# Gate weights on VectorE, staggered first tiles, and value products of 288 and 144 columns in an mLSTM block

## The chip, the cores and the metric

One NeuronCore of a Trainium2 chip runs the whole program. The time is device microseconds of one execution, from the first to the last instruction and what lies around them; 2079.76 us is the median of three runs. TensorE (PE) multiplies, with its weight loads shown apart (PEld), VectorE (DVE), ScalarE (ACT) and GpSimd (POOL) do the elementwise work, and SyncE (SP) issues the DMAs.

## What is computed

Two layers on 1024 latent tokens and 256 context tokens of width 1024. The change lies in the first layer, a bidirectional mLSTM. Its features and gates are, cut to what matters:

```python
xm, z, og = split(h @ w_in, 3)            # h: 1280 tokens x 1024, each part 2048 wide
xc = silu(short_conv(xm, conv_w, conv_b)) # width 3 along the tokens
q = headwise(xc, w_q); k = headwise(xc, w_k) * DH ** -0.5
v = headwise(xm, w_v)                     # blocks of 4 channels
pre = concat(q, k, v) @ w_gate + b_gate   # 16 gate columns: both directions
# then the chunked scans of both directions over 4 heads, norm, gating with z and og, @ w_out
```

The second layer is a pooling mixer; the change does not touch it.

## The kernel before

Float32 accuracy comes from products of two halves: each operand is a high part and a low part in float32r, and mm3 makes high x high, high x low and low x high into one PSUM buffer. So each operand is split: ACT copies the high part, DVE subtracts it from the value for the low part.

**Start.** ada_product and ada_turn make shift and scale for 128 columns of the width at a time; PE_START is the order, written out by hand, of these steps and of the steps F0 to F7. F k is early(k): it modulates column tile k of the normalized input, splits it, and multiplies it with the weights of the first two of 16 feature tiles (n = 0 and 1). Each of the two tiles has three PSUM buffers, for 512, 512 and 256 tokens.

**Feature tiles.** For each n, features(n, side) makes 128 channels of xm: three token chunks of 8 x 3 matmuls. Each chunk is copied to xp for the convolution (L367), its high part to xmh (L369) and its low part to xml (L370); then the convolution (L372 to L374), silu (L375), the split into xch and xcl (L382, L383), and stores. token_part(n) is a generator that features(n+1) and (from n = 1 on: two of them in features(2)) later tiles draw on through `next(side)`, between their own groups of matmuls: after every group for n = 2, after every second one else. A step multiplies 128 tokens of xm with vv, the 128 columns of the block-diagonal v weights and 16 gate columns (144 together), as high and low; three such steps share a PSUM buffer of tag "pb" (two buffers), and ACT and DVE then read it for v's high part (L409), its low part (L410) and the gate sums `pre` (L411). The last step adds the gate products of xch and xcl (tag "pc").

**gate_weights** multiplies the gate weights into the 4x4 blocks of q, k and v and leaves them, split, in gx_all and gm_all; vv takes its 16 columns from gm_all (L397). It is called behind features(1) and runs on POOL; its three tiles of weights are loaded into buffers of tag "T5" (five buffers).

**block_sums** prepares sums of blocks of h for the Strassen products behind the feature tiles. For each of four k it loads two tiles of h_d (L511), forms the sums (L513 to L516), and in four further steps splits one each (L520, L521) and stores it. Two steps are taken behind each feature tile from n = 2 on. All of these tiles, and xmh, xml, xch and xcl, have tag "S4" (32 buffers).

**Order.** PE's order in this stage is the program's. On the other engines and the queues a planner puts the instructions in order before the run, by its own timeline; each engine then works its list in order. Buffers of a tag pass from one tile to the next.

**Plain and Strassen products** for z and og follow (L528 on); the first plain product draws the rest of token_part(15). Then the heads: start_head(0) loads chunk 0 of xh_d and xl_d of the first head (fetch_x), make_A and next_q make q, load_ctx_gates and load_gates fetch the gates' rows, finish_x loads chunks 1 and 2, and fetch_v the values. score_chunk(st, ci) multiplies q with chunk ci.

Of the kernel before, what the change touches and what calls it, by code (L numbers as in the profile page):

```python
# [51 lines left out]
def hybrid_block(ctx: ExitStack, tc: tile.TileContext, xT, ctxT, vecs, w_ada0, w_ada, w_blk, w_krow, blk_mask, w_gate, w_in, b_gate, w_out,  # L52
# [219 lines left out]

    ps_, quad = {}, []

    def early(k):
# [13 lines left out]
        for n in range(2):  # L289
            if k == 0:  # L290
                ps_[n] = [pt_("pc" if n else "pa") for _ in range(3)]
            for ci in range(3):
                mm3(ps_[n][ci][:, :CHUNKS[ci][1]], first_w[n][0][:, k], first_w[n][1][:, k], hx(k, ci, 0), hx(k, ci, 1),
                    k == 0, k == KD - 1)
# [25 lines left out]
    def gate_weights():  # L320
        gsum = tl("T5", [P, 3, KE, 16])

        def add4(dst, src):
            G.tensor_tensor(dst, src[:, :, 0], src[:, :, 1], op=ALU.add)
            for o in (2, 3):
                G.tensor_tensor(dst, dst, src[:, :, o], op=ALU.add)

        for i in range(3):
            g4 = tl("T5", [P, KE, 4, 16])
            nc.sync.dma_start(g4, w_gate[i])  # L330
            G.tensor_tensor(g4, g4, wb[:, i, :, :, None].to_broadcast([P, KE, 4, 16]), op=ALU.mult)
            add4(gsum[:, i], g4)
        G.tensor_scalar(gsum[:, 1], gsum[:, 1], QSCALE, None, op0=ALU.mult)
        G.tensor_tensor(gsum[:, 0], gsum[:, 0], gsum[:, 1], op=ALU.add)
        for dst, i in ((gx_all, 0), (gm_all, 2)):
            G.tensor_copy(dst[:, :, 0:16], gsum[:, i])
            G.tensor_tensor(dst[:, :, 16:32], gsum[:, i], f(dst[:, :, 0:16]), op=ALU.subtract)
# [14 lines left out]
    def features(n, side):  # L352
# [7 lines left out]
        for ci, (o, w) in enumerate(CHUNKS):  # L360
# [9 lines left out]
            V.tensor_tensor(dl, p[:, :w], f(dh), op=ALU.subtract)  # L370
# [18 lines left out]
    def token_part(n, xmh, xml, xch, xcl):  # L389
# [8 lines left out]
        vh, vl = tl("T5", [P, 10, P], F32R), tl("T5", [P, 10, P], F32R)  # L398
        for s0, s1 in ((0, 3), (3, 6), (6, 9), (9, 10)):
            p = pt_("pb", [P, 3, 144])  # L400
            for s in range(s0, s1):
# [5 lines left out]
                mm3(p[:, s - s0], ah, al, vv[:, 0], vv[:, 1], True, True)  # L407
            q = p[:, :s1 - s0]
            S.activation(vh[:, s0:s1], q[:, :, :P], AF.Copy)  # L409
            V.tensor_tensor(vl[:, s0:s1], q[:, :, :P], f(vh[:, s0:s1]), op=ALU.subtract)  # L410
            V.tensor_tensor(pre[:, s0:s1], pre[:, s0:s1], q[:, :, P:], op=ALU.add)  # L411
        for t, dst in ((vh, vh_d), (vl, vl_d)):
            nc.sync.dma_start(dst[n // 4, :, :, (n % 4) * P:(n % 4 + 1) * P], f(t))
# [112 lines left out]
    with ctx0:  # L526
        for n in range(KE):
# [8 lines left out]
            if n >= 2:  # L536
                for _ in range(2):
                    next(sums, None)
# [739 lines left out]
```

## Time and profile before

| | us |
|---|---|
| median of 3 runs (2079.72 to 2080.05) | 2079.76 |
| the profiled execution | 2081.2 |
| its span, first to last instruction | 2079.4 |
| PE busy in the span | 1993.0 (96%) |
| PE busy from 0 to 260 us | 209.6 |
| feature tile without a disturbance | 18.4 |
| feature stage, 88.3 to 393.0 us | 304.7 |

A row of a stretch gives the busy time of each engine, the number of its instructions, and the granted clock of TensorE as a share of full speed (2.4 GHz). A timeline row is start, duration, engine, line, operation, output and inputs, and in brackets how long the engine had been idle before and what ended that. Matmuls overlap; the distance of two starts tells what one costs.

### The profile page before, as it was taken

To read this page: it belongs to the slowest core of one execution; us is meant where nothing else is said; L and a number is where in the kernel's file an instruction comes from. 1 tells how busy PE (TensorE), PEld (TensorE's weight loads), DVE (VectorE), ACT (ScalarE), POOL (GpSimd) and SP (SyncE) were. 2 spreads that over 40 slices of the span, in tenths; PEclk is the share of its full clock that TensorE was granted. 3 is DMA by queue.
4 is the path that set the end of the run, shared out by engine and by line. 5 is a ranking of instruction groups with operands and counts; after the bars stand their busy time and mean duration, and the time that the engine had idled before them with its cause. 6 is when DMAs were issued, how large, how long until landed. Compare 5 with 4: busy or idle time off the path is not lost.

```text
span 2079.4 us, 26941 instructions
## 1 busy us (share of the span) xinstructions
PE 1993.0 (96%) x10210; PEld 1681.9 (81%) x10210; DVE 1232.9 (59%) x2106; ACT 759.7 (37%) x1225; POOL 309.1 (15%) x394
## 2 busy tenths in 40 slices
PE   6779999999999899999999999999999999999998
PEld 4567888878888678888888888887888888888897
DVE  4636666677777666667676572454647283744444
ACT  5424555433333332333323332443423131224443
POOL 1120000033223000000000000252100000000275
PEclk9889999999999999999999999999999999999999
DMA  8347776774443674737447234534331212134573
GB/s 349 125 146 246 252 247 234 246 269 140 136 147 127 209 250 123 254 107 244 137 138 247 94 99 137 175 131 150 122 112 51 96 51 86 57 106 142 174 246 127
DMA packets 201986, 339.48 MB, mean 163 GB/s; under 512 B 12508, under 2 KB 116444, under 8 KB 201856
## 3 DMA queue, kind: packets, MB, share of 16 engines
q1 hardware_dynamic: 201856, 337.76, 48.0%
q8 instruction: 80, 1.31, 0.3%
q14 instruction: 50, 0.41, 0.1%
HBM read 234.77 MB, written 102.94 MB: 162 GB/s over the span
## 4 chain that ended last, share of the span: by engine, by line
PE 84%; DMA 5%; DVE 4%; POOL 3%; issue 2%; ACT 1%; SPq 0%; DVEq 0%; POOLq 0%; ACTq 0%
PE pa L136 43%; PE pc L136 32%; PE pb L136 7%; PE pb L787 1%; DMA wr<-in_w_ada_dram 1%; POOL S L995 1%; POOL hn L975 1%; PE pc L818 1%; DMA S<-in_w_ada_dram 1%; DMA S<-in_ctxT_dram 0%; DVE wl L664 0%; DVE S L907 0%; DMA T<-in_bw_out_dram 0%; DMA S<-xl_d 0%; DVE T L746 0%
## 5 line engine op out<-in xcount | busy, mean ns | idle before, releaser
L136 PE MATMUL pa<-S,wh 128*128 128x512 f32 (+1 forms) x2448 | 709.8, 375 | 5.3 <-DVE pt L370 5.0
L136 PEld LDWEIGHTS pa<-S,wh 128*128 128x128 f32 x2448 | 437.9, 190 | 75.0 <-DVE pt L370 5.6
L136 PE MATMUL pc<-S,wh 128*128 128x512 f32 (+1 forms) x1664 | 464.5, 365 | 3.9 <-ACT wh L142 3.1
L136 PE MATMUL pa<-S,wl 128*128 128x512 f32 (+1 forms) x1224 | 453.5, 371 | 3.9 <-DVE wl L144 3.9
L136 PEld LDWEIGHTS pc<-S,wh 128*128 128x128 f32 x1664 | 301.2, 189 | 55.1 <-ACT wh L142 3.3
L144 DVE TENSOR_TENSOR wl<-wr,wh 128x1024 fp32r<-128x1024 f32 (+1 forms) x124 | 147.3, 1188 | 271.3 <-ACT wh L142 270.4
L136 PE MATMUL pc<-S,wl 128*128 128x512 f32 (+1 forms) x832 | 302.3, 365 | 1.0 <-DVE wl L144 1.0
L136 PEld LDWEIGHTS pa<-S,wl 128*128 128x128 f32 x1224 | 232.4, 190 | 44.8 <-DVE wl L144 4.7
L136 PE MATMUL pa<-S,S 128*128 128x512 f32 (+1 forms) x1152 | 251.1, 363 | 10.0 <-DMA S<-xh_d 6.3
L142 ACT ACTIVATE wh<-wr 128x1024 fp32r<-128x1024 f32 (+1 forms) x124 | 124.7, 1006 | 362.7 <-PE pa L136 142.4
L136 PE MATMUL pc<-S,pt 128*128 128x512 f32 x960 | 227.8, 392 | 1.3 <-DVE S L727 0.9
L136 PEld LDWEIGHTS pa<-S,S 128*128 128x128 f32 x1152 | 191.9, 190 | 40.1 <-DMA S<-xh_d 6.7
L136 PEld LDWEIGHTS pc<-S,pt 128*128 128x128 f32 x960 | 178.4, 188 | 38.4 <-DVE S L727 1.6
L136 PEld LDWEIGHTS pc<-S,wl 128*128 128x128 f32 x832 | 157.3, 189 | 26.6 <-DVE wl L144 1.8
L789 ACT ACTIVATE pt<-pb 128x512 fp32r<-128x512 f32 (+1 forms) x96 | 47.9, 523 | 215.3 <-PE pb L787 209.5
L975 POOL TENSOR_TENSOR hn<-hn,pt 128x512 f32<-128x512 f32 (+1 forms) x48 | 77.5, 1617 | 308.5 <-ACT pt L974 307.4
L746 DVE SCALAR_TENSOR_TENSOR T<-pa,T 128x256 f32<-128x256 f32 (+3 forms) x184 | 78.1, 453 | 33.7 <-PE pa L136 29.5
L136 PEld LDWEIGHTS pb<-vv,S 128*128 128x128 f32 x384 | 62.8, 194 | 37.6 <-issue 26.0
L136 PE MATMUL pb<-vv,S 128*128 128x144 f32 x384 | 59.6, 265 | 27.2 <-DVE vv L397 25.6
L136 PE MATMUL pb<-S,wh 128*128 128x512 f32 x256 | 78.8, 389 | 0.0
L576 ACT ACTIVATE wh<-T 128x512 fp32r<-128x512 f32 x70 | 41.2, 627 | 96.3 <-PE pc L136 78.4
L410 DVE TENSOR_TENSOR T<-pb,T 128x384 fp32r<-128x384 f32 x64 | 31.3, 490 | 72.8 <-ACT T L409 72.7
(323 smaller groups left out, 2317.5 us busy)
## 6 DMA issues: line engine op xcount, KB each, us to landing
wr<-in_bw_in_dram SPq DMA_DIRECT2D x40, 512.0 KB, 3.6
wr<-in_w_in_dram SPq DMA_DIRECT2D x34, 512.0 KB, 4.7
wr<-in_w_ada_dram SPq DMA_DIRECT2D x32, 512.0 KB, 4.2
wr<-in_w_out_dram SPq DMA_DIRECT2D x32, 512.0 KB, 3.6
T<-in_bw_out_dram SPq DMA_DIRECT2D x32, 512.0 KB, 4.6
S<-y_d SPq DMA_DIRECT2D x28, 512.0 KB, 7.1
vh_d<-T SPq DMA_DIRECT2D x16, 640.0 KB, 4.0
vl_d<-T SPq DMA_DIRECT2D x16, 640.0 KB, 5.6
```

The lines of the kernel that those rows point to most:

```text
L136: PE.matmul(out, lhsT, rhs, start=start, stop=stop)
L142: S.activation(h, r, AF.Copy)
L144: V.tensor_tensor(l, r, f(h), op=ALU.subtract)
L410: V.tensor_tensor(vl[:, s0:s1], q[:, :, :P], f(vh[:, s0:s1]), op=ALU.subtract)
L576: S.activation(hi, a, AF.Copy)
L746: V.scalar_tensor_tensor(W[:, lo + sh:hi + sh], p[:, lo - o:hi - o], 1.0, W[:, lo + sh:hi + sh], op0=ALU.mult, op1=ALU.mult, accum_out=dp[ ...
L787: PE.transpose(p[:, j], st["M"][:, s * P:(s + 1) * P], ident)
L789: S.activation(th[:, :n], p[:, :n], AF.Copy)
L818: PE.transpose(p[:, c], hn[:, c * P:(c + 1) * P], ident)
L975: G.tensor_tensor(acc, acc, sq, op=ALU.add)
L995: engs[1].tensor_tensor(t, t, xr[n // per][:, n % per], op=ALU.add)
```

## The change

Six edits. In the start, tile 1 runs four column tiles behind tile 0 and catches up at k = 7. gate_weights is called ahead of features(0) and runs on VectorE. L370 reads xp in place of the PSUM buffer. A value step multiplies the high part of the tokens with both halves of vv at once (288 columns), adds the low part's product to the first half (144 columns), and has a PSUM buffer of its own, copied by ACT; for five token tiles at once DVE then adds the two halves and the gate sums, and v is split and stored. block_sums has a sixth step, ahead of the sums, and three steps are taken per tile up to n = 9. At the start of the heads, chunk 1 of head 0 is fetched right behind chunk 0, and load_gates stands ahead of load_ctx_gates.

```diff
@@ -286,12 +287,17 @@
             parts = [(*pair, slice(0, T))]
         modulate(x_sb[k], rs_xs, parts, k, 0, h_d[k])
         modulate(c_sb[k // 4][:, k % 4], rs_cs, [(hch[k // 4][:, k % 4], hcl[k // 4][:, k % 4], slice(0, TC))], k, 1)
-        for n in range(2):
-            if k == 0:
-                ps_[n] = [pt_("pc" if n else "pa") for _ in range(3)]
-            for ci in range(3):
-                mm3(ps_[n][ci][:, :CHUNKS[ci][1]], first_w[n][0][:, k], first_w[n][1][:, k], hx(k, ci, 0), hx(k, ci, 1),
-                    k == 0, k == KD - 1)
+        feature_step(0, k)
+        for k1 in (k - 4,) if k < KD - 1 else range(3, KD):
+            if k1 >= 0:
+                feature_step(1, k1)
+
+    def feature_step(n, k):
+        if k == 0:
+            ps_[n] = [pt_("pc" if n else "pa") for _ in range(3)]
+        for ci in range(3):
+            mm3(ps_[n][ci][:, :CHUNKS[ci][1]], first_w[n][0][:, k], first_w[n][1][:, k], hx(k, ci, 0), hx(k, ci, 1),
+                k == 0, k == KD - 1)
 
     rows = {}
     for step in PE_START.split():
@@ -321,20 +327,20 @@
         gsum = tl("T5", [P, 3, KE, 16])
 
         def add4(dst, src):
-            G.tensor_tensor(dst, src[:, :, 0], src[:, :, 1], op=ALU.add)
+            V.tensor_tensor(dst, src[:, :, 0], src[:, :, 1], op=ALU.add)
             for o in (2, 3):
-                G.tensor_tensor(dst, dst, src[:, :, o], op=ALU.add)
+                V.tensor_tensor(dst, dst, src[:, :, o], op=ALU.add)
 
         for i in range(3):
             g4 = tl("T5", [P, KE, 4, 16])
             nc.sync.dma_start(g4, w_gate[i])
-            G.tensor_tensor(g4, g4, wb[:, i, :, :, None].to_broadcast([P, KE, 4, 16]), op=ALU.mult)
+            V.tensor_tensor(g4, g4, wb[:, i, :, :, None].to_broadcast([P, KE, 4, 16]), op=ALU.mult)
             add4(gsum[:, i], g4)
-        G.tensor_scalar(gsum[:, 1], gsum[:, 1], QSCALE, None, op0=ALU.mult)
-        G.tensor_tensor(gsum[:, 0], gsum[:, 0], gsum[:, 1], op=ALU.add)
+        V.tensor_scalar(gsum[:, 1], gsum[:, 1], QSCALE, None, op0=ALU.mult)
+        V.tensor_tensor(gsum[:, 0], gsum[:, 0], gsum[:, 1], op=ALU.add)
         for dst, i in ((gx_all, 0), (gm_all, 2)):
-            G.tensor_copy(dst[:, :, 0:16], gsum[:, i])
-            G.tensor_tensor(dst[:, :, 16:32], gsum[:, i], f(dst[:, :, 0:16]), op=ALU.subtract)
+            V.tensor_copy(dst[:, :, 0:16], gsum[:, i])
+            V.tensor_tensor(dst[:, :, 16:32], gsum[:, i], f(dst[:, :, 0:16]), op=ALU.subtract)
 
     gx_all = tl("hn", [P, KE, 32], F32R)
     gm_all = tl("hn", [P, KE, 32], F32R)
@@ -367,7 +373,7 @@
             S.activation(xp[:, xo:xo + w], p[:, :w], AF.Copy)
             dh, dl = (xmh[0][:, o:o + w], xml[0][:, o:o + w]) if ci < 2 else (xmh[1], xml[1])
             S.activation(dh, p[:, :w], AF.Copy)
-            V.tensor_tensor(dl, p[:, :w], f(dh), op=ALU.subtract)
+            V.tensor_tensor(dl, xp[:, xo:xo + w], f(dh), op=ALU.subtract)
         y = tl("T5", [P, 1281])
         S.activation(y, xp[:, 1:1282], AF.Identity, scale=vc("conv_w", 16 + n), bias=vc("conv_b", n))
         V.scalar_tensor_tensor(y, xp[:, 0:1281], vc("conv_w", n), y, op0=ALU.mult, op1=ALU.add)
@@ -395,22 +401,24 @@
         V.tensor_copy(vv[:, 0, :P], bv)
         V.tensor_tensor(vv[:, 1, :P], bv, f(vv[:, 0, :P]), op=ALU.subtract)
         V.tensor_copy(vv[:, :, P:], f(gm_all[:, n]).rearrange("p (a b) -> p a b", a=2))
-        vh, vl = tl("T5", [P, 10, P], F32R), tl("T5", [P, 10, P], F32R)
-        for s0, s1 in ((0, 3), (3, 6), (6, 9), (9, 10)):
-            p = pt_("pb", [P, 3, 144])
-            for s in range(s0, s1):
+        for s0 in (0, 5):
+            vst, vhl = tl("T5", [P, 2, 5, 144]), tl("T5", [P, 2, 5, P], F32R)
+            for s in range(s0, s0 + 5):
                 yield
                 if s < 8:
                     ah, al = xmh[0][:, s * P:(s + 1) * P], xml[0][:, s * P:(s + 1) * P]
                 else:
                     ah, al = xmh[1][:, (s - 8) * P:(s - 7) * P], xml[1][:, (s - 8) * P:(s - 7) * P]
-                mm3(p[:, s - s0], ah, al, vv[:, 0], vv[:, 1], True, True)
-            q = p[:, :s1 - s0]
-            S.activation(vh[:, s0:s1], q[:, :, :P], AF.Copy)
-            V.tensor_tensor(vl[:, s0:s1], q[:, :, :P], f(vh[:, s0:s1]), op=ALU.subtract)
-            V.tensor_tensor(pre[:, s0:s1], pre[:, s0:s1], q[:, :, P:], op=ALU.add)
-        for t, dst in ((vh, vh_d), (vl, vl_d)):
-            nc.sync.dma_start(dst[n // 4, :, :, (n % 4) * P:(n % 4 + 1) * P], f(t))
+                p = pt_("pb", [P, 2, 144])
+                mm(p.rearrange("p a b -> p (a b)"), ah, vv.rearrange("p a b -> p (a b)"), True, False)
+                mm(p[:, 0], al, vv[:, 0], False, True)
+                S.activation(vst[:, :, s - s0], p, AF.Copy)
+            V.tensor_tensor(vst[:, 0], vst[:, 0], vst[:, 1], op=ALU.add)
+            V.tensor_tensor(pre[:, s0:s0 + 5], pre[:, s0:s0 + 5], vst[:, 0, :, P:], op=ALU.add)
+            S.activation(vhl[:, 0], vst[:, 0, :, :P], AF.Copy)
+            V.tensor_tensor(vhl[:, 1], vst[:, 0, :, :P], f(vhl[:, 0]), op=ALU.subtract)
+            for t, dst in ((vhl[:, 0], vh_d), (vhl[:, 1], vl_d)):
+                nc.sync.dma_start(dst[n // 4, :, s0:s0 + 5, (n % 4) * P:(n % 4 + 1) * P], f(t))
         yield
 
         gx = gx_all[:, n]
@@ -509,6 +517,7 @@
             t0, t1 = tl("S4", [P, T]), tl("S4", [P, T])
             for t, kk in ((t0, k), (t1, k + 4)):
                 nc.sync.dma_start(t, h_d[kk])
+            yield
             b11, b12, b21, b22 = t0[:, :512], t0[:, 512:], t1[:, :512], t1[:, 512:]
             V.scalar_tensor_tensor(b22, b22, dsh[:, k], b12, op0=ALU.add, op1=ALU.subtract)
             V.tensor_tensor(b12, b12, b11, op=ALU.subtract)
@@ -524,17 +533,17 @@
 
     side, parts, sums = iter(()), [], block_sums()
     with ctx0:
+        gate_weights()
         for n in range(KE):
             out = features(n, side)
             for _ in side:
                 pass
             if n == 1:
                 gacc.extend(pt_("pc") for _ in range(3))
-                gate_weights()
             if n == 2:
                 bilinear()
             if n >= 2:
-                for _ in range(2):
+                for _ in range(3 if n < 10 else 2):
                     next(sums, None)
             parts.append(token_part(n, *out))
             if n:
@@ -839,10 +848,11 @@
             fetch_x(cur["hd"], cur["h"], ci)
 
     cur = start_head(0)
+    fetch_x(cur["hd"], 0, 1)
     cur["A"] = make_A(0)
     cur["q"] = next_q(cur, 0)
-    cur["rc"], cur["R"] = load_ctx_gates(0), load_gates(0)
-    finish_x(cur)
+    cur["R"], cur["rc"] = load_gates(0), load_ctx_gates(0)
+    fetch_x(cur["hd"], 0, 2)
     fetch_v(cur["hd"], 0, 0, 5)
     st_prev = st_now = nxt = None
     for i in range(len(seq) + 1):
```

## Rows read from the trace of the kernel before

**Rows 1.** Page, part 1: busy us (share) and instructions of each engine.

```profile
PE 1993.0 (96%) x10210; PEld 1681.9 (81%) x10210; DVE 1232.9 (59%) x2106; ACT 759.7 (37%) x1225; POOL 309.1 (15%) x394
```

**Rows 2.** Waits of PE, whole run: us in total, times, longest.

```profile
PE pb L136 <- DVE vv L397: 25.6, 1, 25.6
...
PE pa L136 <- DMA S<-xh_d: 6.3, 1, 6.3
...
PE pa L136 <- DMA S<-xl_d: 1.9, 1, 1.9
...
PE pa L136 <- DVE S L727: 1.8, 1, 1.8
```

**Rows 3.** Stretches: busy us per engine, PEclk, DMA share, GB/s.

```profile
88.30:139.80 51.50, 25.35 (x144) 21.13 (x145) 24.97 (x42) 17.59 (x29) 18.45 (x24) 0.73 0.43 149
...
158.20:184.40 26.20, 22.44 (x111) 18.34 (x110) 16.18 (x30) 11.94 (x22) 0.15 (x3) 0.87 0.57 202
...
239.80:261.00 21.20, 18.37 (x108) 15.51 (x106) 11.82 (x23) 9.95 (x16) 0.15 (x3) 0.98 0.82 264
261.00:282.50 21.50, 21.45 (x109) 18.20 (x110) 13.27 (x26) 10.32 (x18) 0.15 (x3) 0.86 0.56 205
...
337.80:356.20 18.40, 18.40 (x109) 15.82 (x108) 10.52 (x21) 9.22 (x17) 0.16 (x3) 1.00 0.58 200
```

**Rows 4.** Timeline of POOL: first and last operation of gate_weights.

```profile
96.88 2.32 POOL L331 TENSOR_TENSOR T<-T,cst 128x1024 f32<-128x1024 f32 x1 [54.34 <-ACT S L382]
...
115.30 0.72 POOL L337 TENSOR_TENSOR hn<-T,hn 128x256 fp32r<-128x256 f32 x1
```

**Rows 5.** Timeline of DVE, 67 to 87 us: the two longest idle times.

```profile
70.74 0.17 DVE L507 TENSOR_TENSOR dsh<-mod 128x4 f32<-128x4 f32 x1 [3.23 <-ACT mod L195]
...
86.39 0.69 DVE L370 TENSOR_TENSOR S<-pa,S 128x512 fp32r<-128x512 f32 x1 [10.89 <-ACT S L369]
```

**Rows 6.** Timeline of PE in feature tile 13.

```profile
339.67 0.62 PE L136 MATMUL pa<-S,wh 128*128 128x512 f32 x2
...
340.35 0.45 PE L136 MATMUL pb<-vv,S 128*128 128x144 f32 x3
...
342.07 0.45 PE L136 MATMUL pb<-vv,S 128*128 128x144 f32 x3
...
351.36 0.40 PE L136 MATMUL pa<-S,wh 128*128 128x256 f32 x2
...
351.72 0.46 PE L136 MATMUL pb<-vv,S 128*128 128x144 f32 x3
```

**Rows 7.** Groups by line and form, 337.8 to 356.2: busy, mean ns, idle before.

```profile
L409 ACT ACTIVATE T<-pb 128x384 fp32r<-128x384 f32 x3 | 1.5, 490 | 4.0 <-PE pb L136 4.0
L372 ACT ACTIVATE T<-T,vec 128x1281 f32<-128x1281 f32 x1 | 1.5, 1462 | 0.0
...
L383 DVE TENSOR_TENSOR S<-T,S 128x1024 fp32r<-128x1024 f32 x1 | 1.2, 1224 | 0.3 <-ACT S L382 0.3
```

**Rows 8.** Timelines around the end of tile 8: DVE, ACT, then PE.

```profile
257.69 0.75 DVE L513 SCALAR_TENSOR_TENSOR S<-S,dsh,S 128x512 f32<-128x512 f32 x1 [0.80 <-DMA S<-h_d]
...
264.31 0.68 DVE L370 TENSOR_TENSOR S<-pa,S 128x512 fp32r<-128x512 f32 x1
...
261.69 0.63 ACT L520 ACTIVATE S<-S 128x512 fp32r<-128x512 f32 x1 [1.81 <-DVE S L515]
262.23 1.06 ACT L369 ACTIVATE S<-pa 128x512 fp32r<-128x512 f32 x2
...
261.05 1.22 PE L136 MATMUL pa<-S,wh 128*128 128x512 f32 x2 [2.89 <-DVE pt L370]
```

**Rows 9.** Timelines of SP, ACT and PE at the start of the heads.

```profile
719.91 1.22 SPq L683 DMA_DIRECT2D S<-xh_d  x2
...
724.44 0.40 ACT L761 ACTIVATE T<-S,cst 128x128 f32<-128x128 f32 x1 [0.96 <-DMA S<-a_d]
...
727.85 0.79 PE L136 MATMUL pa<-S,S 128*128 128x512 f32 x1 [6.29 <-DMA S<-xh_d]
```

## The prediction

> **What bounds the kernel now.** I read the page first: TensorE (PE) is busy 96% of the span [rows 1], so time can only come from PE's idle time, from stretches at the lower clock, or from shorter PE work. The waits of PE, longest first, come next: one wait of 25.6 us for `vv` at L397, then 6.3 and 1.9 us for loads of `xh_d` and `xl_d`, 1.8 us for L727 [rows 2]. The view by stretches places them. From 88.3 to 139.8 us (`features(2)` runs in it) PE works 25.35 of 51.5 us at a granted clock of 0.73. A tile without disturbance takes 18.4 us, all of it busy. Three stretches are longer: 26.2, 21.2 and 21.5 us [rows 3]. The rest of the first stage is saturated, and so is nearly everything behind it.
>
> **The 25.6 us.** PE's first value product needs `vv`, `vv` needs `gm_all`, and that is the last thing that gate_weights makes. On POOL it runs from 96.88 to 116.0 us [rows 4], because it is issued behind the work of tile 1. The change puts it ahead of tile 0 and on VectorE (DVE). Its three products of 1024 columns cost there what a 1024-column subtraction costs, 1.22 us; the other 15 operations have 256 columns, and I take a third of that, 0.42 us, each (between 0.31, in proportion to columns, and 0.72, POOL's own time in rows 4): 3 x 1.2 + 15 x 0.4 = 9.6 us [rows 4, 7]. Its cover is DVE's idle time of 3.2 and 10.9 us in 67 to 86 us and smaller gaps before [rows 5]; the three 512 KB loads need only the T5 buffers of the first ada weights, used up by then. Queued behind each of these operations is the modulation of a coming column tile, delayed by one operation, 1.2 us at most; the stagger leaves these tiles several microseconds before PE asks for them, as PE does only half of its work for k below 4 and makes it up at k = 7. If the cover is gone, 9.6 us fall on the path (third rival).
>
> The stagger takes no work from PE. It ends tile 0 five groups of nine matmuls early, so that tile 0's evictions run beside tile 1's products. I give it 0.8 us, for the start of `features(2)`, between 0 and 2.
>
> What is late next in that stretch? Its PE work at full clock is 16 groups of three 512-column matmuls at 0.68, 8 groups of 256 columns at 0.36, 20 value groups at 0.25 (below) and two sets of gate products at what is left of an undisturbed tile, 18.4 - 10.9 - 2.9 - 10 x 0.36 = 1.0: 10.9 + 2.9 + 5.0 + 2.0 = 20.8 us [rows 3, 6]. ScalarE (ACT) has in the same time two conv chains, three tiles' evictions and 20 new small ones, about 22 us, and its order puts tile 1's evictions before the first value eviction; I add a stall of 3.5 us (0 to 8). So 51.5 - 24.3 + 0.8 = **28 us** saved (23 to 32), the low clock behind the wait included.
>
> **Value products.** A step with a value group takes 342.07 - 340.35 = 1.72 us; two groups of three 512-column matmuls without one take 2 x 0.68 = 1.36. So three 144-column matmuls cost 0.36 us, 0.12 each, as much as one of 256 columns (0.36 for three) [rows 6]. A matmul this narrow thus pays a floor, and the change pays it twice instead of three times: 288 columns at 0.12 + 32 x (0.227 - 0.12)/256 = 0.13, and 144 at 0.12, together 0.25. There are 160 groups, 20 already counted: 140 x 0.10 = **14 us** (the 288 columns at the price of 256 would give 17; at that of 512, 0.23, nothing).
> The trace fits a floor set by the weight load: the Trainium skill ("TensorE: Matmul & The Clock Gate", section "LDWEIGHTS (loading the stationary operand)") gives a time that goes with the weight's columns alone, an estimate of 107 ns for 128. The same page of the Trainium skill, section "Back-to-back issue gap", has a rule that speaks against the change: the gap goes by the moving columns plus 2.5 ns. By that rule 432 columns stay 432 and the edit is worth an estimated 0.4 us in all. The 0.36 us in rows 6, where columns alone would make about 0.19, is against it.
>
> **New evictions.** Each group now has a PSUM buffer of its own (two of them), read by one ACT copy. A 384-column copy takes 0.49 us [rows 7]; 288 columns cost less, I take 0.41. Per tile ACT gains ten of these and two splits of about 0.7, and loses 1.8: some 4 us on 9.2 busy of 18.4 [rows 3]. DVE's net is about +1 us on 10.5. Neither becomes the bound on average. But the third group ahead must wait for the copy: PE leaves 1.4 us of other work between groups, and ACT's longest instruction, the conv at L372, takes 1.46 us [rows 6, 7]. Where the groups are dense (tile 15's, beside the first plain products) I expect 2.5 us of waits, and 1.5 over the other tiles: **-4 us** (0 to -12).
>
> **PSUM read by ACT only, and block_sums.** The two slow spots cost 26.2 - 18.4 = 7.8 and 21.2 + 21.5 - 36.8 = 5.9 us [rows 3]. In the second, PE waits until 261.05 for L370, whose buffer the 256-column chunk holds; with L370 reading `xp`, that buffer is free when ACT is done, some 2 us sooner. But the row behind it is worse: the copy L369 into `xmh` runs at 262.23, right behind L520, which waited for L515, and all of it for the `h_d` loads that arrive at 257.69; L370 then makes `xml` at 264.31 [rows 8]. L369 stands behind L520 since S4 tiles are given out in program order, and this batch of block_sums steps holds both a load and the first split of it. Two of the old batches do that (n = 2, 7). With six steps a turn, three a tile, every even n from 2 to 8 does: load, sums, first split. The new yield changes nothing in this, as both steps are taken in one batch. PE asks for both about 3 us into the next tile; in rows 8 `xml` begins to come 6.1 us after PE had run out of the tile before (261.05 - 2.89 = 258.16). I price four stalls at 4.5 us each, waits and lower clock together (the old ones cost 7.8 and 5.9, less what the early buffer saves; bounds 1 and 7): 13.7 - 18 = **-4.3 us** (+10 to -14).
>
> **Start of the heads.** The chunk-1 loads of head 0 are issued at 719.91, and PE waits for them 6.3 and 1.9 us [rows 2, 9]. Moved ahead of A, q and the gates they take the S4 buffers that the last Strassen products free, and so can be issued while those still run; what is moved behind them (the context gates, chunk 2) is wanted later. The gates' rows, which arrive at 724.44, then set the end: without them no score leaves its PSUM buffer, and each of the three buffers is filled by twelve 512-column matmuls, 2.7 us [rows 6, 9]. Of 8.2 us I expect **5.7** back (2 to 8.2).
>
> **Sum.** 28 + 14 - 4 - 4.3 + 5.7 = 39.4 us. The profiled execution took 2081.2 us (span 2079.4), 1.4 above the median of the runs, 2079.76; 39.4 off it is 2041.8, and on the median's scale 2040.
>
> **Rivals.**
> First, slower: ACT's copies bind. Each value group waits for the copy two groups back, because ACT sits in a conv instruction or in a wait for DVE ahead of it. Place: all 160 groups; price at 0.4 us each 64 us, so 2104. It turns the sign from 39.4/160 = 0.25 us a group. For it: two buffers, ACT in order, 1.46 us instructions [rows 7]. Against it: half of ACT's time is free in a tile [rows 3], and the 1.4 us between groups nearly covers its longest instruction.
> Second: narrow matmuls cost by columns, and the merge saves nothing: 16 us less, 2056. Rows 6 speak against it; only a 288-column matmul, which the trace does not hold, could show otherwise. It is the rule of the page of the Trainium skill named above.
> Third: the move of gate_weights does not do what it says, since DVE runs it behind the conv work of tiles 0 and 1; `vv` is then ready near 100 us and PE still waits about 12: 2052. For it: the modulations of k = 4 to 7 share these gaps. Against it: 10.9 us of them come in one piece before the first eviction [rows 5].
>
> **How the numbers follow.** Forecast 0.72, slower rival 0.08, columns 0.10, late gates 0.10. The forecast's own spread is 2025 to 2055, mostly from the four stalls, the evictions and the stretch to 139.8. To leave no more than 2 in 10 out, the range takes in the second and third rivals with a few microseconds of that spread: 2021 to 2061. A difference below about 0.2% (4 us) cannot be told from none. Faster by more 0.89, within 0.03, slower by more 0.08.
>
> **What would show it.** Right: no wait for `vv`, `features(2)` over near 112 us; value steps of 1.61 us; POOL idle there; stalls of PE on L369 or L370 in the first microseconds of tiles 4, 6, 8 and 10; PE working on chunk 1 near 721 us. Wrong: PE waiting for the new copy in most tiles, steps still at 1.72 us, DVE's gate work past 88 us, or no stall at all in those four tiles (then it is near 2022).

## The result, and the profile after

| | before | after |
|---|---|---|
| median, us | 2079.91 | 2062.1 (2061.25 to 2063.37) |
| ratio to before | | 0.9915, 95% interval 0.9897 to 0.9932 |
| profiled execution, us | 2081.2 | 2062.4 |
| its span, us | 2079.4 | 2060.7 |

The change makes the kernel 0.85% faster. 18.7 us of the profiled span are gone, where the prediction's sum had 39.4; the median lies 1 us above the predicted range.

The page of after, part 1, answers [rows 1]:

```profile
PE 1982.7 (96%) x10050; PEld 1668.4 (81%) x10050; DVE 1258.9 (61%) x2092; ACT 809.4 (39%) x1353; POOL 289.5 (14%) x376
```

PE has 160 matmuls and 10.3 us of work less, ACT has 50 us more. The waits of PE in after (us in total, times, longest) answer [rows 2]:

```profile
PE pb L136 <- ACT S L375: 14.5, 4, 4.0
...
PE pb L136 <- DVE S L376: 7.1, 4, 1.8
PE pb L136 <- ACT T L415: 6.3, 5, 2.4
PE pa L136 <- DMA S<-xh_d: 5.0, 1, 5.0
...
PE pa L136 <- ACT pt L375: 1.7, 4, 0.4
```

The 25.6 us for `vv` are gone. In their place stand three groups of four waits each: the copies into `xmh` (L375, in before L369), the low part `xml` (L376, in before L370), and the copy of the 256-column chunk into a tile of tag "pt" (L375 too). The new copy of a value group (L415) costs 6.3 us, and chunk 2 of head 0 costs 5.0.

The stretches of after (length, busy time of PE, PEld, DVE, ACT and POOL, granted clock, DMA share, GB/s) answer [rows 3]. The first is `features(2)`, the other three are `features(4)`, `features(5)` and `features(6)`:

```profile
88.30:113.90 25.60, 20.23 (x115) 16.41 (x114) 16.61 (x27) 19.23 (x40) 0.00 (x0) 1.00 0.68 234
...
131.78:158.19 26.41, 20.57 (x101) 16.69 (x98) 18.15 (x29) 15.74 (x29) 0.33 (x6) 0.87 0.75 264
158.19:175.73 17.54, 17.54 (x101) 14.95 (x98) 10.57 (x17) 11.37 (x21) 0.00 (x0) 1.00 0.66 212
175.73:202.55 26.82, 20.61 (x101) 16.71 (x98) 18.15 (x29) 15.74 (x29) 0.33 (x6) 0.87 0.71 253
```

A tile without disturbance takes 17.54 us (18.4 before). Four tiles, 4, 6, 8 and 10, take 26.41, 26.82, 26.57 and 26.58: 36.2 us over four undisturbed ones. In the first of them PE idles 26.41 - 20.57 = 5.8 us and works 20.57 - 17.54 = 3.0 us longer, most of it by the lower clock (granted 0.87 over the tile); over the four it is 5.5 to 6.2 and 3.0 to 3.5 us.

One of these stalls in the timelines, in the order PE, DVE, ACT:

```profile
177.47 0.73 PE L136 MATMUL pa<-S,wh 128*128 128x512 f32 x2 [0.42 <-ACT pt L375]
...
184.49 0.40 PE L136 MATMUL pb<-vv,S 128*128 128x288 f32 x1 [4.01 <-ACT S L375]
...
186.68 0.49 PE L136 MATMUL pb<-vv,S 128*128 128x144 f32 x1 [1.78 <-DVE S L376]
...
178.74 0.75 DVE L522 SCALAR_TENSOR_TENSOR S<-S,dsh,S 128x512 f32<-128x512 f32 x1 [0.62 <-DMA vl_d<-T]
...
182.55 0.74 DVE L524 SCALAR_TENSOR_TENSOR S<-S,mod,S 128x512 f32<-128x512 f32 x1
...
185.94 1.28 DVE L376 TENSOR_TENSOR S<-T,S 128x512 fp32r<-128x512 f32 x2
...
183.33 0.63 ACT L529 ACTIVATE S<-S 128x512 fp32r<-128x512 f32 x1 [3.94 <-DVE S L524]
183.86 1.07 ACT L375 ACTIVATE S<-pa 128x512 fp32r<-128x512 f32 x2
```

This is the chain of [rows 8], once in every second tile. DVE begins the sums (L522) at 178.74 and has the third of them, behind a conv instruction, at 182.55. ACT waits for that one with the first split (L529), and only behind it makes both copies into `xmh`; DVE's `xml` comes at 185.94, PE's value products at 184.49 and 186.68. The line L375 writes two chunks at once here: both had been held back. The releaser that the L522 row names is a store of v; of the two `h_d` loads the second, issued at 171.61, landed 7.1 us later, which is when the sums begin. ACT's copy of the 256-column chunk, into "pt", runs at 177.04, ahead of the split; only the two copies into tiles of tag "S4" stand behind it. That fits the prediction's reason, S4 tiles given out in program order; no run takes the tag apart from the rest of ACT's order.

### The profile page after: what moved, and what is told of

It is laid out like the page before. It is cut to its first block, busy times and chain, and to the rows that moved or that the text cites. A ratio compares the mean times of both kernels' runs of the same rounds, so it can differ in the third digit from the quotient of the medians.

```text
span 2060.7 us, 26787 instructions
## 1 busy us (share of the span) xinstructions
PE 1982.7 (96%) x10050; PEld 1668.4 (81%) x10050; DVE 1258.9 (61%) x2092; ACT 809.4 (39%) x1353; POOL 289.5 (14%) x376
## 4 chain that ended last, share of the span: by engine, by line
PE 86%; DVE 5%; DMA 5%; ACT 2%; issue 1%; SPq 0%; POOL 0%; DVEq 0%; ACTq 0%; POOLq 0%
PE pa L136 43%; PE pc L136 34%; PE pb L136 7%; PE pb L796 1%; DMA wr<-in_w_ada_dram 1%; PE pc L827 1%; DMA S<-in_w_ada_dram 1%; DVE S L917 1%; DMA S<-in_ctxT_dram 0%; DMA vl_d<-T 0%; DVE wl L673 0%; DMA T<-in_bw_out_dram 0%; DMA S<-xh_d 0%; DMA cst<-in_w_blk_dram 0%; DVE wl L144 0%
## 5 line engine op out<-in xcount | busy, mean ns | idle before, releaser
L798 ACT ACTIVATE pt<-pb 128x512 fp32r<-128x512 f32 (+1 forms) x96 | 47.8, 524 | 211.8 <-PE pb L796 202.7
L755 DVE SCALAR_TENSOR_TENSOR T<-pa,T 128x256 f32<-128x256 f32 (+3 forms) x184 | 78.1, 453 | 35.9 <-PE pa L136 31.4
L136 PEld LDWEIGHTS pb<-vv,S 128*128 128x128 f32 x256 | 48.3, 194 | 40.3 <-ACT S L375 16.2
L415 ACT ACTIVATE T<-pb 128x288 f32<-128x288 f32 x160 | 62.9, 412 | 43.2 <-PE pb L136 42.7
L136 PE MATMUL pb<-vv,S 128*128 128x288 f32 (+1 forms) x256 | 50.1, 276 | 27.0 <-ACT S L375 14.5
```

Of the source, the lines that this page charges most:

```text
L136: PE.matmul(out, lhsT, rhs, start=start, stop=stop)
L415: S.activation(vst[:, :, s - s0], p, AF.Copy)
L755: V.scalar_tensor_tensor(W[:, lo + sh:hi + sh], p[:, lo - o:hi - o], 1.0, W[:, lo + sh:hi + sh], op0=ALU.mult, op1=ALU.mult, accum_out=dp[ ...
L798: S.activation(th[:, :n], p[:, :n], AF.Copy)
```

## The experiments

They were timed on three other chips, where before took 2080.4 to 2082.6 us, so medians are compared by their ratio to before. PE reached the end of `features(2)` anywhere from 112.6 to 117.7 us in runs whose code is the same up to there: its first feature product starts at 44.9 to 48.5 us, and from there it takes 67.6 to 69.2 us. What a tile costs is therefore read from the distance of two marks in one trace (the starts of PE's gate products of one tile and of the next), which repeats to 0.1 us in undisturbed tiles.

**One step, then three.** Is it the place of the load in its batch of block_sums steps?

```diff
-                for _ in range(3 if n < 10 else 2):
+                for _ in range(1 if n == 2 else 3):
```

> One number of the changed kernel is altered: the first feature tile that draws on block_sums (n = 2) takes one step, all later ones three, so the load of h_d is taken one feature tile ahead of its sums and of the first split. Theory (the high-part copy of the next tile stands behind the first split of a batch that also holds its own load, and that costs some 9 us in each of tiles 4, 6, 8 and 10): the four stalls go, 36 us less than the changed kernel, near 2026 us, and tiles 4, 6, 8, 10 take about 17.6 us each, like the others. Rival (the long tiles come from the new PSUM copies on ScalarE and the added work of VectorE, whatever batch the load stands in): the time stays within 3 us of 2062, and the waits for the high-part copy stay.

Measured: 2036.6 us, ratio 0.978 (0.9761 to 0.980). Tiles 4, 6, 8 and 10 take 18.9, 19.9, 19.5 and 19.7 us; from the end of `features(2)` to that of the value products 28.4 of the 36 us are gone. Timelines of DVE and ACT, and the stretch of `features(6)`:

```profile
171.24 0.75 DVE L522 SCALAR_TENSOR_TENSOR S<-S,dsh,S 128x512 f32<-128x512 f32 x1 [1.92 <-DMA S<-h_d]
...
162.95 0.61 ACT L375 ACTIVATE S<-pa 128x512 fp32r<-128x512 f32 x1
...
165.30 0.60 ACT L375 ACTIVATE S<-pa 128x512 fp32r<-128x512 f32 x1
...
168.30:188.16 19.86, 18.05 (x101) 14.94 (x98) 15.22 (x25) 13.16 (x25) 0.16 (x3) 1.00 0.86 310
```

The sums begin 171.24 - 168.30 = 2.9 us into the tile, in after 178.74 - 175.73 = 3.0: the load is as late as it was. But the copies into `xmh` run at 162.95 and 165.30, in the tile before, since no split of that batch stands ahead of them any more. So it is the order of ACT's list, not the load as such. The theory holds for 28 of 36 us, and the rival does not; 1.4 to 2.3 us a tile stay, mostly as waits for the copy of a value group.

**Two steps everywhere.** Load and sums in one batch, no split behind them:

```diff
-                for _ in range(3 if n < 10 else 2):
+                for _ in range(2):
```

> The changed kernel with two steps of block_sums behind every feature tile: each load of h_d then shares its batch with its sums, and no split stands behind a load in the same batch. This parts the two ways in which a late load can reach the copies. Theory (the high-part copy is held up by a split ahead of it on ScalarE that waits for the load): no tile near 26.5 us; the 36 us come back but for 1.5 to 2.5 us in each of the four tiles behind a batch of load and sums, 2030 to 2034 us. Rival (it is the sums, waiting for the load on VectorE ahead of the low-part copy, that make the long tiles): four tiles of 24 to 27 us remain, 2055 to 2062.

Measured: 2035.2 us, ratio 0.9773 (0.9748 to 0.9799). No tile is longer than 19.4 us. Two of the four stretches behind a batch of load and sums, and DVE's first and third sum of the second:

```profile
135.60:154.50 18.90, 17.76 (x100) 15.02 (x98) 15.31 (x26) 13.49 (x25) 0.17 (x3) 1.00 0.85 295
189.54:208.57 19.03, 17.80 (x101) 15.01 (x98) 15.21 (x25) 13.27 (x25) 0.16 (x3) 1.00 0.77 273
...
191.65 0.75 DVE L522 SCALAR_TENSOR_TENSOR S<-S,dsh,S 128x512 f32<-128x512 f32 x1 [1.09 <-DMA S<-h_d]
...
196.74 0.75 DVE L524 SCALAR_TENSOR_TENSOR S<-S,mod,S 128x512 f32<-128x512 f32 x1
```

DVE waits for the load here, and the third sum comes 7.2 us into the tile, later than in after (6.8), yet the tile costs 1.5 us too much, not 9. Sums that wait on DVE do little harm; a split that waits on ACT ahead of the copies does the harm.

**One step, then two.** Both remedies at once, and the less work in a batch:

```diff
-                for _ in range(3 if n < 10 else 2):
+                for _ in range(1 if n == 2 else 2):
```

> One step of block_sums behind the first feature tile that draws on it, two behind each later one: load a tile ahead of the sums, and never more than sums and one split in a batch. In the run with one step and then three, the tiles behind sums and two splits kept 1.4 to 2.3 us each, waiting for the copy of a value group's PSUM buffer. Theory (these are ScalarE and VectorE work on top of a full list, so less of it per batch costs less): the four tiles keep 0 to 1.2 us each, 3 to 7 us better than that run, about 2030 us. Rival (they come from the late load itself): the same 1.4 to 2.3 us in four tiles, 2034 to 2036.

Measured: 2035.7 us, ratio 0.9772 (0.9752 to 0.9792); against the run with three steps no difference can be told. The tiles keep 1.4 us each, 5.5 in all instead of 7.8, always with one wait of the same size:

```profile
202.78 0.47 PE L136 MATMUL pb<-vv,S 128*128 128x288 f32 x2 [1.14 <-ACT T L415]
```

So neither forecast holds whole: part of the rest goes with the work per batch and a part does not; what sets the 1.14 us was not taken further. This version beats before and after.

**block_sums of before.**

```diff
             for t, kk in ((t0, k), (t1, k + 4)):
                 nc.sync.dma_start(t, h_d[kk])
-            yield
...
-                for _ in range(3 if n < 10 else 2):
+                for _ in range(2):
```

> The changed kernel with block_sums as it was before: two steps behind each feature tile, the load and the sums in one step. By the theory only the batches behind n = 2 and n = 7 hold a load and its first split, so two long tiles remain of four (tiles 4 and 9): 2 x 9 = 18 us less than the changed kernel, near 2044 us. By the rival (the new copies and VectorE's load make the tiles long) it stays within 3 us of 2062.

Measured: 2053.0 us, ratio 0.9856 (0.9834 to 0.9877). The two long tiles stand where the theory puts them, 4 and 9:

```profile
132.35:158.95 26.60, 20.66 (x100) 16.70 (x98) 17.54 (x28) 15.21 (x28) 0.33 (x6) 0.87 0.70 244
...
231.36:257.71 26.35, 20.83 (x100) 16.80 (x98) 17.45 (x28) 15.21 (x28) 0.33 (x6) 0.87 0.69 239
```

They cost 26.60 + 26.35 - 2 x 17.54 = 17.9 us; tiles 6 and 11 keep 2.3 and 1.4. The new yield and the third step thus doubled the number of stalls; without them the change would have gained some 12 us more (0.9915 - 0.9856 = 0.0059 of 2080), of the 18 that the theory gave.

**VectorE reads PSUM again.**

```diff
-            V.tensor_tensor(dl, xp[:, xo:xo + w], f(dh), op=ALU.subtract)
+            V.tensor_tensor(dl, p[:, :w], f(dh), op=ALU.subtract)
```

> The changed kernel with VectorE again reading the low part out of the PSUM buffer instead of xp. The prediction took it that the earlier free buffer saves some 2 us in each stalled tile: then four tiles get 2 us longer each, 2070 us, and PE's wait for that buffer rises from 0.42 to some 2.5 us. Rival (PE in these tiles waits for the high part of the tokens anyway, so an earlier buffer only moves the wait): the four long tiles stay at 26.4 to 26.8 us and the time within 2 us of 2062.

Measured: 2062.1 us, ratio 0.9915 (0.9885 to 0.9945): the rival. PE in `features(6)`, and its stretch:

```profile
179.42 0.73 PE L136 MATMUL pa<-S,wh 128*128 128x512 f32 x2 [2.83 <-DVE pt L376]
...
184.03 0.40 PE L136 MATMUL pb<-vv,S 128*128 128x288 f32 x1 [1.59 <-ACT S L375]
...
186.21 0.33 PE L136 MATMUL pb<-vv,S 128*128 128x144 f32 x1 [1.78 <-DVE S L376]
...
175.28:199.77 24.49, 18.29 (x100) 14.92 (x98) 18.13 (x29) 15.62 (x29) 0.33 (x6) 1.00 0.78 276
```

The later buffer adds 2.4 us to the first wait and takes 2.4 off the second: both end on the same chain. The sum is 6.2 us with either, so the early buffer takes nothing off the waits of a stalled tile. This one is shorter, 24.49 us, as its clock did not fall; the other three take 26.2, 25.7 and 26.5 (more on this in the last section).

**Three products of 144 columns**, with the new buffers and evictions:

```diff
-                mm(p.rearrange("p a b -> p (a b)"), ah, vv.rearrange("p a b -> p (a b)"), True, False)
-                mm(p[:, 0], al, vv[:, 0], False, True)
+                mm(p[:, 0], ah, vv[:, 0], True, False)
+                mm(p[:, 0], al, vv[:, 0], False, True)
+                mm(p[:, 1], ah, vv[:, 1], True, True)
```

> The changed kernel with three products of 144 columns in each value group again, in the same PSUM buffer and with the same evictions; only the 288-column product is parted. Theory (a product this narrow pays a floor of about 0.12 us): an undisturbed feature tile is 10 x 0.09 to 0.10 = 0.9 to 1.0 us longer (18.4 to 18.5 against 17.54), the whole 14 us longer, 2076. Rival (the cost goes by columns, and the shorter tile has another reason, such as the evictions of PSUM): tile of 17.5 to 17.6 us, 2062.

Measured: 2077.9 us, ratio 0.9986 (0.9974 to 0.9998). An undisturbed and a stalled tile:

```profile
160.93:179.35 18.42, 18.42 (x110) 15.82 (x108) 10.67 (x18) 11.60 (x21) 0.00 (x0) 1.00 0.72 233
...
134.40:160.93 26.53, 21.14 (x110) 17.42 (x108) 18.06 (x30) 15.80 (x29) 0.33 (x6) 0.87 0.74 258
```

Ten more matmuls a tile cost 18.42 - 17.54 = 0.88 us, 0.09 each, at an unchanged number of columns: the floor of [rows 6], and the evictions have no part in it. The Trainium skill ("TensorE: Matmul & The Clock Gate", section "Back-to-back issue gap") gives its rule by columns for a matmul by itself and says that it counts too little where the columns are few, a reservation that the prediction does not name. By the rule alone the ten matmuls would add an estimated 0.03 us; the trace does not agree with that, by these 0.88 us, and bears out the reservation.

The second row needs care. The stalled tile takes 26.53 us with the longer products as well (the other three 26.2, 28.3 and 26.6), 26.41 without them, and 26.2 in before [rows 3]. That does not put PE's work inside the chain over DVE and ACT. The chain ends with the low part's first product, 10.2 us behind the tile's mark here and 10.6 in after; what PE does behind it takes 14.4 us in an undisturbed tile here and 13.5 in after, but 16.3 and 15.9 in these two. So the longer work is there, and less time at the lower clock hides it.

**gate_weights early, on GpSimd.**

```diff
-            V.tensor_tensor(g4, g4, wb[:, i, :, :, None].to_broadcast([P, KE, 4, 16]), op=ALU.mult)
+            G.tensor_tensor(g4, g4, wb[:, i, :, :, None].to_broadcast([P, KE, 4, 16]), op=ALU.mult)
```

(and so each operation of gate_weights)

> The changed kernel with gate_weights left at its new place ahead of the first feature tile, but on GpSimd as before. Theory (the place is what counts: GpSimd needs some 19 us for it and has little to do before 88 us): no wait for the value weights, within 3 us of the changed kernel, 2062. Rival (the engine counts): the value weights come late again, a wait of PE of 10 to 25 us behind 88 us, 2072 to 2086.

Measured: 2074.8 us, ratio 0.996 (0.9947 to 0.9972). Neither theory: PE has no wait for `vv`, and yet `features(2)` ends 12.6 us later than in after (2.5 of it stood already at 42 us, ahead of GpSimd's first gate operation). Timelines of DVE and POOL:

```profile
58.72 2.15 DVE L264 SCALAR_TENSOR_TENSOR S<-S,gs,hn 128x256 f32<-128x256 f32 x1
60.80 2.02 DVE L398 TENSOR_TENSOR bv<-mask,cst 128x128 f32<-128x128 f32 x1
...
58.10 4.57 POOL L337 TENSOR_TENSOR T<-T,cst 128x1024 f32<-128x1024 f32 x2 [9.01 <-DMA T<-in_w_gate_dram]
```

Between 42 and 76 us the 128-column operation of L398 takes 0.93 us on average (three of them), in after 0.28, and the 256-column one of L264 takes 0.91 against 0.47. PE waits 10.0 us from 42 us on for ACT's copies of the ada rows (L187; 3.0 in after), and works 24.2 us in this stretch against 31.0: the start runs late, by some 10 us in all.

**gate_weights late, on VectorE.**

```diff
     with ctx0:
-        gate_weights()
...
                 gacc.extend(pt_("pc") for _ in range(3))
+                gate_weights()
```

> The changed kernel with gate_weights called behind the second feature tile again, but on VectorE. With the run that keeps the early place on GpSimd this parts place from engine. Theory (late is costly on either engine, as its loads wait for T5 buffers of the first tiles until near 96 us, and some 10 us of work follow): the value weights come near 106 to 112 us, PE waits 13 to 20 us for them, 2076 to 2084. Rival (VectorE alone is enough, as it runs them at once): a wait under 5 us, 2062 to 2067.

Measured: 2081.0 us, ratio 1.0004 (0.9993 to 1.0015). DVE's first product and last subtraction, and PE's wait:

```profile
93.45 1.22 DVE L337 TENSOR_TENSOR T<-T,cst 128x1024 f32<-128x1024 f32 x1
...
108.16 0.75 DVE L343 TENSOR_TENSOR hn<-T,hn 128x256 fp32r<-128x256 f32 x2
...
109.27 0.70 PE L136 MATMUL pb<-vv,S 128*128 128x288 f32 x2 [19.69 <-DVE vv L403]
```

`features(2)` ends 18.3 us later than in after. So late on VectorE costs 18 us, as the theory had it, and early on GpSimd 10: place and engine are both needed.

**No stagger.**

```diff
         feature_step(0, k)
-        for k1 in (k - 4,) if k < KD - 1 else range(3, KD):
-            if k1 >= 0:
-                feature_step(1, k1)
+        feature_step(1, k)
```

> The changed kernel without the stagger of the first two tiles: both advance column tile by column tile, as before. The prediction gave the stagger 0.8 us (0 to 2) at the end of the first tiles: then 2062 to 2064, with the first value products 1 to 2 us later. Rival (VectorE is now full from 42 to 76 us with the gate weights, and it is the stagger that lets PE work on meanwhile): PE waits for the modulated column tiles before 80 us, and the time is 5 us longer or more, 2067 and up.

Measured: 2066.4 us, ratio 0.9938 (0.9915 to 0.9960), which by the times alone can't be told from after. From PE's first feature product to the end of `features(2)` it takes 71.3 us, against 67.6 to 69.2 in the runs with the stagger: worth some 2 to 4 us, above the 0.8 (0 to 2) given to it. The longer of those runs have the same waits as the shorter ones, and a granted clock of 0.93 to 0.94 over the stretch of the value products, as this run has, so some 1.4 us need not be the stagger's. PE has no wait for modulated tiles before 80 us; it waits at 87 to 89 us for weights and at 95 us for the copies of value groups, 3.4 us there against 2.4:

```profile
95.10 0.73 PE L136 MATMUL pb<-vv,S 128*128 128x288 f32 x2 [3.38 <-ACT T L413]
```

That fits the prediction's reason, tile 0's evictions out of the way, with a larger price; the rival's reason is not there.

**Start of the heads as before.**

```diff
-    fetch_x(cur["hd"], 0, 1)
...
-    cur["R"], cur["rc"] = load_gates(0), load_ctx_gates(0)
-    fetch_x(cur["hd"], 0, 2)
+    cur["rc"], cur["R"] = load_ctx_gates(0), load_gates(0)
+    finish_x(cur)
```

> The changed kernel with the start of the heads as it was before: chunk 1 of head 0 fetched behind A, q and both kinds of gates, context gates first. Theory (the earlier chunk 1 is worth 6.45 us of the gain, read from the two traces): 2068 to 2069 us, with waits of PE of about 6 and 2 us for the chunk-1 loads. Rival (the gain there belongs to something else, such as the state of the queues behind the shorter feature tiles): within 2 us of 2062.

Measured: 2066.2 us, ratio 0.9922 (0.9897 to 0.9946), which can't be told from after. In the trace, PE at the start of the heads:

```profile
705.04 2.46 PE L136 MATMUL pa<-S,S 128*128 128x512 f32 x6 [1.79 <-DVE S L736]
...
712.93 0.80 PE L136 MATMUL pa<-S,S 128*128 128x512 f32 x1 [3.05 <-DMA S<-xh_d]
...
715.63 2.93 PE L136 MATMUL pa<-S,S 128*128 128x512 f32 x6 [1.90 <-DMA S<-xl_d]
```

The wait for chunk 1 is 3.05 us, not the 6.29 of [rows 9], with the same order of the code. From PE's first q product to the first transpose of a store (L827, in before L818) it takes 55.1 us in before, 51.6 here and 48.7 in after: between these traces 3.0 of 6.4 us go with the new order and 3.5 with the earlier edits. But after is the shortest of ten runs with its order, which take 48.7 to 51.0 us, so the order is worth 0.6 to 3.0 us. SP issued these loads 4.3 us behind the first q product here, 6.3 in before, since a store ahead of them held its queue for 1.07 us instead of 2.89; why, was not tried.

**Chunk 2 earlier.** Both on top of the run with one step, then two. First ahead of the gates' rows, then right behind chunk 1:

```diff
-    cur["R"], cur["rc"] = load_gates(0), load_ctx_gates(0)
     fetch_x(cur["hd"], 0, 2)
+    cur["R"], cur["rc"] = load_gates(0), load_ctx_gates(0)
```

> As the run with one step and then two, and chunk 2 of head 0 fetched ahead of both kinds of gates, behind A and q. PE's wait for chunk 2 is 5.0 us in the changed kernel. Theory (chunk 2 is late because its loads are issued behind the gates' rows, 2.6 us): the wait falls to 2 to 3 us, 2 to 3 us better than the run without this. Rival (the gates' rows then come later and the scores cannot leave PSUM): a new wait of the same size on the vector work behind the scores, no gain.

```diff
     fetch_x(cur["hd"], 0, 1)
+    fetch_x(cur["hd"], 0, 2)
     cur["A"] = make_A(0)
...
-    fetch_x(cur["hd"], 0, 2)
```

> As the run with one step and then two, and chunk 2 of head 0 fetched right behind chunk 1, ahead of A and q. Theory (its buffers are free while the last Strassen products run): no wait for chunk 2, 4 to 5 us better than the run without this. Rival (the buffers come free only with these products, and SyncE's queue stands still on them with the gates' rows and A behind): chunk 2 no earlier than 3 us before now, gates later, a gain of 0 to 2 us or a loss.

Measured: 2033.4 us, ratio 0.9765 (0.9746 to 0.9784), and 2037.0, ratio 0.978 (0.9761 to 0.9799): neither can be told from the run without them (0.9772). PE's longest wait at the start of the heads, chunk 2 last, ahead of the gates, and first:

```profile
686.56 2.04 PE L136 MATMUL pa<-S,S 128*128 128x256 f32 x5 [4.91 <-DMA S<-xh_d]
```

```profile
685.87 2.50 PE L136 MATMUL pa<-S,S 128*128 128x512 f32 x5 [2.50 <-DVE T L755]
```

```profile
689.60 2.93 PE L136 MATMUL pa<-S,S 128*128 128x512 f32 x6 [4.96 <-DVE T L755]
```

The wait changes its name. With chunk 2 earlier, the scores can't leave PSUM, since L755 needs what ACT makes of the gates' rows: 2.5 us, beside 2.0 and 0.5 for chunk 2 in the first of the two, 5.0 in the second. In the first ACT waits for the rows themselves. In the second it stands before that with a copy of q (L735), for which it waits 7.6 us for PE, so the rows are not the only reason there. By the waits the first run's rival was right; a small gain is there all the same: from the first q product to the first transpose of a store the two take 47.8 and 47.9 us, 49.4 in the run without them and 48.7 to 51.0 in the ten runs with the order of after.

## Why the prediction was wrong

The 20.7 us between the sum and the trace, term by term (gain predicted, gain measured between marks of PE's timeline):

| term | predicted | measured |
|---|---|---|
| to the end of `features(2)` | 28 | 24.4 |
| value products behind it | 14 | 12.3 |
| new evictions behind it | -4 | -1.4 |
| stalls of block_sums | -4.3 | -22.6 |
| gates' chain behind tile 15 | | -2.8 |
| start of the heads | 5.7 | 6.4 |
| later | | 2.3 |
| sum | 39.4 | 18.6 |

Each row compares one execution of either kernel. In the other runs whose code is the same in that part, the first row comes out at 20.6 to 25.7 us, the gates' chain at -0.3 to -1.1, the heads at 4.1 to 6.3 and the last at -1.6 to 2.8. What after shows in the last three rows is partly chance; the stalls are not.

**The step that failed is the price of the four stalls.** That there would be four, in tiles 4, 6, 8 and 10, and through L520 ahead of L369, was right, and the runs with other steps show that it is this order. Each was priced at 4.5 us, between 1 and 7; they cost 8.9 to 9.3, of which 5.5 to 6.2 are waits of PE. Two things made the price too low. First, the chain was read in [rows 8], where `xml` begins 6.1 us behind PE's last work on the tile before. That is the quicker of the two old stalls: the sums begin there 0.8 us behind the tile's mark (257.69). In the other, in tile 4 of before (timeline of DVE), they begin 2.3 us behind it, and `xml` 8.1 us behind PE's last work, which ends at 158.4:

```profile
159.41 0.74 DVE L513 SCALAR_TENSOR_TENSOR S<-S,dsh,S 128x512 f32<-128x512 f32 x1
...
166.49 1.28 DVE L370 TENSOR_TENSOR S<-pa,S 128x512 fp32r<-128x512 f32 x2
```

The four in after are like this one: 2.3 to 3.0, and 8.2 to 8.9 us. Second, the early buffer was to save part of it, and takes nothing off the waits (VectorE on PSUM again: the same 6.2 us). A price read from the length of the longer old stall, 26.2 - 17.5 = 8.7, would have given 13.7 - 4 x 8.7 = -21 and a time near 2057. That it comes so close is luck in part: in that old tile PE waited 26.20 - 22.44 = 3.8 us and worked 4.0 longer than in an undisturbed one [rows 3], in after 5.8 and 3.0.

**To the end of `features(2)`.** No wait for `vv`, the gate work done by 73.7 us, POOL idle: as forecast. The last gate operation on DVE, and three value steps of PE in `features(12)`, in after:

```profile
72.98 0.75 DVE L343 TENSOR_TENSOR hn<-T,hn 128x256 fp32r<-128x256 f32 x2
...
315.48 0.37 PE L136 MATMUL pb<-vv,S 128*128 128x288 f32 x2
317.11 0.37 PE L136 MATMUL pb<-vv,S 128*128 128x288 f32 x2
318.74 0.37 PE L136 MATMUL pb<-vv,S 128*128 128x288 f32 x2
```

PE waits 5.4 us for the new copies (2.4, 1.8, 0.3 and 0.9) where 3.5 were given; its work from 87.7 us to the end of the gate products is 22.2 us, not 20.8; and the stretch begins 0.6 us sooner, not 0.8. These make the 3.6. The cover of the gate work was there, but thin: DVE is busy 32.0 of the 34 us from 42 to 76.

**Value products.** From one value step to the next it takes 1.63 us (318.74 - 317.11; 1.72 in [rows 6]), 1.61 was forecast: 0.09 a group instead of 0.10. The rival of the columns is refuted by the parted product.

**New evictions.** No wait for them in an undisturbed tile, 0.9 us in the dense part of tile 15, where ten groups take 0.6 us longer than before instead of 0.9 shorter: 1.4 us. ACT copies in 0.41 us, as taken. They bind only where something else delays ACT or DVE: in `features(2)` and in the 1.4 to 2.3 us that the tiles behind the sums keep. So the slower rival's mechanism is there, at the 6.3 us of waits of the whole run in place of 64.

**Gates' chain**, not in the prediction. Behind tile 15 PE waits for L499 (in before, the same transposes come without a wait), and the stretch behind that has a low clock, of which before has none there:

```profile
424.78 0.65 PE L504 MATMUL pb<-ident,T 36*128 36x36 f32 x8 [0.86 <-DVE T L499]
...
425.50:433.00 7.50, 7.50 (x31) 6.09 (x30) 6.03 (x6) 2.33 (x4) 7.23 (x5) 0.77 0.61 175
```

The transposes stand 33.1 us behind the mark of tile 15, 31.8 in before. What made them late was not tried. From that mark to the first q product it takes 309.2 us in before, 311.9 in after and 309.4 to 310.3 in the twelve other runs, so most of the 2.8 us belongs to this execution.

**Heads.** The sum is near, 5.7 against 6.4, its reason at most half so: the order is worth 0.6 to 3.0 us, and the chunk-1 wait is replaced by 5.0 us for chunk 2, of which the two other orders take off little.

## What to carry to other kernels

A step that waits for its own load can hold back later work of its engine that does not need the load, as the split held the copies into `xmh` here: put the load, or the load and the sums, a batch ahead of the first such step, before adding more steps. Price a stall by the whole length of a stalled stretch less the undisturbed one, time at the lower clock included, and from the longest stall in the trace as well as the shortest. Beside each wait removed, ask what the same bytes or the same engine will make late instead.

## What the runs showed of the hardware

**GpSimd holds VectorE up.** With GpSimd at its 1024-column products of two SBUF tiles (4.57 us for two), DVE operations of 128 and 256 columns last 2.0 and 2.2 us, nearly the length of one GpSimd product, in place of 0.28 and 0.47. The Trainium skill ("SBUF — State Buffer", section "SBUF: two separate sides") says that the two share a pair of ports, for VectorE operations with two inputs in SBUF such as these, which one instruction holds to its end while the other is blocked; the trace agrees for VectorE as the blocked one.

**The same waits, with and without a fall of the clock.** With VectorE on PSUM, PE waits 2.83, 1.59 and 1.78 us in `features(6)` and 2.27, 1.59 and 1.78 in `features(10)` of the same run. The first tile is granted 1.00 and takes 24.49 us (its row stands above); the second is granted 0.87 and takes 26.53:

```profile
260.57:287.10 26.53, 20.89 (x101) 16.89 (x98) 18.15 (x30) 15.72 (x29) 0.33 (x6) 0.87 0.73 257
```

From the first value product to the end of `features(2)`, where their code is the same, after and the run with two steps everywhere both wait 2.41, 1.8, 0.28 and 0.86 us for the new copies. The stretch in after, then in the other:

```profile
89.12:113.88 24.76, 19.39 (x111) 15.73 (x109) 16.59 (x27) 18.39 (x39) 0.00 (x0) 1.00 0.71 241
```

```profile
91.50:117.70 26.20, 20.83 (x110) 16.94 (x109) 16.68 (x27) 18.39 (x39) 0.00 (x0) 0.93 0.67 228
```

So nearly the same waits cost 1.4 to 2.0 us more or less, by whether the clock falls behind them. What decides that, no run here shows.
